# Three edits to a hybrid decoder block: attention emitted by pairs of query blocks, four weight sums moved to VectorE, a convolution split by token halves

## The chip, the cores and the metric

The kernel runs on one core of a Trainium2 chip. The metric is device microseconds of one execution; the runs before the change took 2504.47, 2507.64 and 2510.67 us, median 2507.64 us.

## The reference

One layer over 2048 tokens of width 1024, float32. What the change touches:

```python
hn = rmsnorm(x, g_mix);  proj = hn @ w_in            # LRU branch, gate branch, q, k, v
# causal depthwise convolution of width 4, then the recurrence with two block-diagonal gates
xc = sum(conv_w[k] * shift(x_lru, 3 - k) for k in range(4)) + conv_b
gate_r, gate_i = sigmoid(xc @ w_a + b_a), sigmoid(xc @ w_x + b_x)
h_t = a_t * h_{t-1} + sqrt(1 - a_t**2) * (gate_i * xc)_t;   y_lru = h * gelu(g_lru)
# attention: 16 heads of 64, blocks of 128 queries against the current and previous 128 keys, a sink per head
y_attn = softmax_with_sink(q @ k.T / 8, window=128) @ v
x = x + concat(rmsnorm(y_lru), rmsnorm(y_attn)) @ w_out
# squared-ReLU MLP
x = x + relu(rmsnorm(x) @ w_up)**2 @ w_down;   out = rmsnorm(x)
```

## The kernel before

The tokens are worked off in two chunks of 1024. A chunk goes through the input projection and attention, the recurrent group (LRU), the output projection, and the first half of the MLP; the second half of the MLP (w_down) follows for all tokens at the end. Matrix products take each float32 operand as a high part rounded by ScalarE (ACT) and a low part that VectorE (DVE) subtracts, so that a product is three TensorE (PE) matmuls: high-high, high-low, low-high. The MLP products use seven instead of eight block products, with sums of weight blocks and of activation blocks as operands.

The order of instructions on each engine is made at build time by a planner: it takes the instructions in the order in which the Python code emits them as their priority, simulates the engines with costs of its own, and gives each engine, when it is free, the ready instruction of highest priority. On the chip each engine then keeps that order and waits wherever its next instruction isn't ready. So the emission order sets priorities; it isn't the queue itself.

**Attention** (the loop over `s`, line 811 on). Step `s` makes the scores of head `s` and the probabilities and values of head `s-1`. A head has four pairs of query blocks. `scores(p)` does 4 matmuls into one of two PSUM buffers (`bank(0, ...)`, L629), DVE mixes the two key blocks (L637), takes the maximum (L639, L640), and ACT makes two exponentials (L643), which frees the buffer. `probs(p)` does 2 transposes (L662), ACT copies (L665), DVE subtracts (L666), GpSimd (POOL) masks twice (L669, L671). `values(p)` does 12 small matmuls (L686). `piece` is a quarter or an eighth of the projection of the next q, x or gate tile, the filler between them. Before the change the step runs in two halves: scores of two pairs, values of two pairs, probabilities of two pairs, two pieces.

**LRU.** For each of eight channel tiles `j`, `lru_a` convolves: ACT scales the two token halves of the projection (L740), DVE adds three shifted taps for each half (L747, L749), copies the last three columns aside (`halo`, L751), then ACT makes the high part `xhi` of all 1024 tokens (L754) and DVE the low part `xlo` (L755). `lru_b` multiplies both by the gate weights (L916 to L918), half by half.

**First half of the MLP.** `Up.run` starts pairs 0 and 1 of weight tiles together: two products each, then `sums()` (L364 to L368, with high parts by ACT L359 and low parts by DVE L360) makes the activation operands T4, T3, T1, then the rest of pair 0 and the rest of pair 1. `weight_sums` makes four half-width sums of the weights on POOL (L395 to L398), then splits them (L400 to L407). For pair 1 it is emitted behind the second of pair 0's remaining products.

Of the kernel before, what the change touches and what calls it, by code (L numbers as in the profile page):

```python
# [9 lines left out]
F32R = mybir.dt.float32r  # L10
# [3 lines left out]
AF = mybir.ActivationFunctionType  # L14
ALU = mybir.AluOpType
# [22 lines left out]
def hybrid_block_kernel(  # L38
# [16 lines left out]
    act = nc.scalar  # L55
    dve = nc.vector
# [18 lines left out]
    def f32(ap):  # L75
        return ap.bitcast(F32)
# [10 lines left out]
    def S(tag, name, dt=F32, shape=(P, D)):  # L87
        return slots.tile(list(shape), dt, name=name, tag=tag)

    def U(i, name, dt=F32, shape=(P, D)):  # L90
        return S(f"u{i}", name, dt, shape)
# [13 lines left out]
    def W(name, dt=F32R, shape=(P, D)):  # L105
        turn["w"] = (turn["w"] + 1) % 5
        return S(f"w{turn['w']}", name, dt, shape)
# [20 lines left out]
    HS = (slice(0, HALF), slice(HALF, D))  # L128
# [37 lines left out]
    def split_weight(src, at=None, eng=None, raw=None):  # L166

        if raw is None:
            raw = R("wraw")
            nc.sync.dma_start(raw, src)  # L170
        if at is None:
            hi, lo = W("whi"), W("wlo")
        else:
            hi, lo = U(at[0], "whi", F32R), U(at[1], "wlo", F32R)
        act.activation(hi, raw, AF.Copy)  # L175
        (eng or dve).tensor_tensor(lo, raw, f32(hi), op=ALU.subtract)  # L176
        return hi, lo
# [116 lines left out]
    pool = nc.gpsimd  # L294
    C_TAGS = ("u0", "u1", "u12")

    class Up:
# [91 lines left out]
            else:  # L389
                self.raws = r1, r2  # L390

        def weight_sums(self, fp, r1, r2):
            lo, hi = slice(0, HALF), slice(HALF, D)
            s12 = U(10, "s12", F32, (P, 2, HALF))
            pool.tensor_tensor(s12[:, 0], r2[:, lo], r2[:, hi], op=ALU.add)  # L395
            pool.tensor_tensor(s12[:, 1], s12[:, 0], r1[:, lo], op=ALU.subtract)
            pool.tensor_tensor(r2[:, lo], r1[:, lo], r2[:, lo], op=ALU.subtract)
            pool.tensor_tensor(r1[:, hi], r1[:, hi], s12[:, 1], op=ALU.subtract)  # L398
            s12h, s12l = W("s12h", F32R, (P, 2, HALF)), W("s12l", F32R, (P, 2, HALF))
            act.activation(s12h, s12, AF.Copy)  # L400
            dve.tensor_tensor(s12l, s12, f32(s12h), op=ALU.subtract)
            f2h, f2l = W("f2h"), U(20, "f2l", F32R)
            act.activation(f2h, r2, AF.Copy)  # L403
            dve.tensor_tensor(f2l, r2, f32(f2h), op=ALU.subtract)  # L404
            s4 = U(21, "s4", F32R, (P, 2, HALF))
            act.activation(s4[:, 0], r1[:, hi], AF.Copy)
            dve.tensor_tensor(s4[:, 1], r1[:, hi], f32(s4[:, 0]), op=ALU.subtract)  # L407
            self.ws[fp] |= {"S2": (s12h[:, 1], s12l[:, 1]), "S1": (s12h[:, 0], s12l[:, 0]),
                            "S3": (f2h[:, lo], f2l[:, lo]), "A22": (f2h[:, hi], f2l[:, hi]),
                            "S4": (s4[:, 0], s4[:, 1])}  # L410
# [66 lines left out]
        def run(self, ahead=None):  # L477
            c = self.c
            first = [self.pair(0), self.pair(1)]
            for i in range(2):  # L480
                if i == 1:
                    self.weights(1)
                for _ in range(2):
                    next(first[i])
            self.sums()
            for i in range(2):
                for n, _ in enumerate(first[i]):
                    if i == 0 and n == 1:
                        self.weight_sums(1, *self.raws)
                    if i == 1 and n == 0:  # L490
                        self.weights(2)
            steps = None
            for fp in range(2, NF // 2):
                for n, _ in enumerate(self.pair(fp, fp + 1 == NF // 2 and c + 1 < NCH)):
                    if n == 1 and fp + 1 < NF // 2:
                        self.weights(fp + 1)
                    if fp + 1 == NF // 2 and c + 1 < NCH:
                        if n == 0:
                            hn, steps = stage1(c + 1)
                        if n in (0, 2, 3, 4, 6):  # L500
                            next(steps)
                        if n == 4:
                            self.wkv = [split_weight(w_in[KT * 3 + i], at=(16 + 2 * i, 17 + 2 * i))
                                        for i in range(2)]
                    if ahead:
                        ahead(fp, n)
            self.next = (hn, steps) if steps else (None, None)
# [15 lines left out]
    for c in range(NCH):  # L523
# [204 lines left out]
        def lru_a(j, xps):  # L728
            def vcol(i):
                return vec[:, i, j:j + 1]  # L730

            wgr = small.tile([P, 2, HD], F32, name="wgr", tag="wgr", bufs=2)
            nc.sync.dma_start(wgr, w_gate[j])
            for s in range(2):
                s_ = slice(s * HD, s * HD + HD)
                act.activation(gd[s_, 0, :, s_], wgr[s_], AF.Copy)
                dve.tensor_tensor(gd[s_, 1, :, s_], wgr[s_], f32(gd[s_, 0, :, s_]), op=ALU.subtract)
            xc = U((16, 20)[j % 2], "xc")
            for n in range(2):
                act.activation(xc[:, HS[n]], xps[n], AF.Identity, scale=vcol(V_CW + 3), bias=vcol(V_CB))  # L740
            for n in range(2):
                before = xps[0][:, HALF - 3:] if n else halo[:, j, :]
                h0 = n * HALF
                for d in (1, 2, 3):
                    w = vcol(V_CW + 3 - d)
                    a_, b_ = slice(h0 + d, h0 + HALF), slice(h0, h0 + d)
                    dve.scalar_tensor_tensor(out=xc[:, a_], in0=xps[n][:, :HALF - d], scalar=w, in1=xc[:, a_],  # L747
                                             op0=ALU.mult, op1=ALU.add)
                    dve.scalar_tensor_tensor(out=xc[:, b_], in0=before[:, 3 - d:], scalar=w, in1=xc[:, b_],  # L749
                                             op0=ALU.mult, op1=ALU.add)  # L750
            dve.tensor_copy(halo[:, j, :], xps[1][:, HALF - 3:])  # L751
            xhi = U((17, 21)[j % 2], "xhi", F32R)
            xlo = U(18, "xlo", F32R)
            act.activation(xhi, xc, AF.Copy)  # L754
            dve.tensor_tensor(xlo, xc, f32(xhi), op=ALU.subtract)  # L755
            return [xc, xhi, xlo]

        def new_x(j):
# [39 lines left out]
        qs, yqs, heads, muls = {}, {}, {}, []  # L798
        pf_next = [0]
        late = []  # L800
        piece, done = new_q(0)
# [4 lines left out]
        piece, done = new_q(1)  # L806
# [4 lines left out]
        for s in range(NH + 1):  # L811
            j = s // 2

            free = mm("tp", (s + 1) // 2 % 2) if 0 < s < NH - 1 else None
            if s < NH:
                if s % 2 == 0:
                    yqs[j] = U(3 + j % 2, "yq", F32, (P, NT, P))
                heads[s] = Head(s, qs[j][s % 2], yqs[j])
            if s % 2 == 1:
                if j + 2 < KT:  # L820
                    piece, done = new_q(j + 2)
                else:
                    piece, done = (new_x if j + 2 == KT else new_gate)(0)

            for p0 in (0, 2):
                if s < NH:
                    for p in (p0, p0 + 1):
                        heads[s].scores(p)
                    if p0:
                        heads[s].sums()  # L830
                if len(late) == 4:
                    for _ in range(2):
                        heads[late[0][0]].values(late.pop(0)[1])
                if s > 0:
                    for p in (p0, p0 + 1):
                        heads[s - 1].probs(p, free)
                        late.append((s - 1, p))
                    if p0 and s % 2 == 1 and s > 1:
                        flip(j - 1, yqs[j - 1])
                for p in (p0, p0 + 1):  # L840
                    piece(p if s % 2 else 4 + p)
            if s % 2 == 1 and j + 2 < KT:
                done(0)
            if s % 2 == 0:
                if j + 1 < KT:
                    qs[j + 1] = done(1)
                elif j + 1 == KT:
                    lru_in = done()
                else:
                    lru_in.append(done())  # L850
# [121 lines left out]
        for grp in range(2):  # L972
# [5 lines left out]
            for k0, kn in (((0, 3), (3, 3), (6, 2)), ((0, 4), (4, 4)))[grp]:  # L978
# [6 lines left out]
                for t in range(NT):  # L985
                    n, tt = divmod(t, NT // 2)
# [336 lines left out]
```

## Time and profile before

| what | us |
|---|---|
| median of the three runs | 2507.64 |
| the profiled execution | 2507.72 |
| its span, first to last instruction | 2506.0 |
| PE busy | 2421.7 |
| DVE busy | 1762.8 |
| ACT busy | 1263.7 |
| POOL busy | 443.1 |

The span is what the profiler saw; the execution's time is 1.7 us longer. An engine's busy time excludes waits. PE is busy nearly all the time, so a change shows in the time only through PE's waits, through its granted clock, or through work that it does more or less of.

### The profile page before, as it was taken

What the parts mean: (1) busy time and instruction counts of PE and PEld (TensorE: products, weight loads), DVE (VectorE), ACT (ScalarE), POOL (GpSimd) and SP (SyncE); (2) the same over time, 40 slices, a digit from 0 to 9 for tenths busy, and PEclk for the clock granted to TensorE, in tenths of its full rate; (3) what the DMA queues carried; (4) which work ended last, traced back from release to release, by engine and by line L of the source; (5) the groups of instructions that cost most, each with busy time, mean ns of one, the idle gap of its engine ahead of it and who ended that gap; (6) DMA issues with size and microseconds to landing.
All of it is one profiled execution on the core that took longest, in us unless ns stands there. A gap on an engine that the chain in (4) does not pass through costs nothing. (4 is left out here: it accounts for less than half of the span.)

```text
span 2506.0 us, 32828 instructions
## 1 busy us (share of the span) xinstructions
PE 2421.7 (97%) x12338; PEld 1974.9 (79%) x12338; DVE 1762.8 (70%) x2534; ACT 1263.7 (50%) x2149; POOL 443.1 (18%) x455
## 2 busy tenths in 40 slices
PE   7999999999999999999999999999999999999997
PEld 6877777788788888877777788788878877888886
DVE  6788667856754556777676847655564898887888
ACT  6666777513455456665778315455454233322334
POOL 0344000001223210544000001423210110111100
PEclk9999999999999999999999999999999999999999
DMA  4111112412344444011113312444463454443424
GB/s 156 42 44 52 45 46 78 152 51 82 129 148 152 163 154 140 35 51 52 46 37 115 112 43 110 147 142 152 162 204 122 155 162 156 135 132 121 135 90 162
DMA packets 132815, 276.39 MB, mean 110 GB/s; under 512 B 11184, under 2 KB 70576, under 8 KB 132656
## 3 DMA queue, kind: packets, MB, share of 16 engines
q1 hardware_dynamic: 124880, 246.50, 29.3%
q0 software_dynamic: 5184, 18.88, 2.1%
q10 hardware_dynamic: 2592, 8.91, 0.9%
q8 instruction: 97, 1.59, 0.3%
q14 instruction: 62, 0.51, 0.1%
HBM read 190.37 MB, written 83.89 MB: 109 GB/s over the span
## 5 line engine op out<-in xcount | busy, mean ns | idle before, releaser
L1240 DVE TENSOR_TENSOR acc<-dd,acc 128x1024 f32<-128x1024 f32 x212 | 256.4, 1218 | 84.0 <-PE dd L1231 83.3
L997 PE MATMUL ops<-whi,ht 128*128 128x512 f32 x1024 | 280.0, 391 | 2.5 <-DVE halo L751 1.3
L1029 ACT ACTIVATE ah<-araw 128x1024 fp32r<-128x1024 f32 x96 | 102.0, 1063 | 299.3 <-PE dd L1231 286.7
L997 PEld LDWEIGHTS ops<-whi,ht 128*128 128x128 f32 x1024 | 191.3, 188 | 45.9 <-DVE x L1002 2.7
L997 PE MATMUL ops<-wlo,ht 128*128 128x512 f32 x512 | 159.2, 391 | 0.0
L669 POOL TENSOR_SCALAR_AFFINE_SELECT pf<-pf 128x512 f16<-128x512 f16 x128 | 89.0, 695 | 348.3 <-DVE pf L666 340.0
L175 ACT ACTIVATE whi<-wraw 128x1024 fp32r<-128x1024 f32 x84 | 88.5, 1055 | 120.6 <-PE ops L997 85.2
L404 DVE TENSOR_TENSOR f2l<-wraw,f2h 128x1024 fp32r<-128x1024 f32 x32 | 39.1, 1223 | 143.7 <-ACT f2h L403 143.7
L1030 DVE TENSOR_TENSOR al<-araw,ah 128x1024 fp32r<-128x1024 f32 x96 | 124.3, 1296 | 10.7 <-ACT ah L1029 10.7
L176 DVE TENSOR_TENSOR wlo<-wraw,whi 128x1024 fp32r<-128x1024 f32 x84 | 103.4, 1235 | 40.4 <-PE xps L234 14.5
L395 POOL TENSOR_TENSOR s<-wraw 128x512 f32<-128x512 f32 x32 | 41.5, 1296 | 500.9 <-DMA wraw<-in_w_up_dram 264.6
L643 ACT ACTIVATE st<-sc,mx 128x128 f32<-128x128 f32 x256 | 91.0, 366 | 62.8 <-DVE mx L640 62.1
L997 PEld LDWEIGHTS ops<-wlo,ht 128*128 128x128 f32 x512 | 95.6, 188 | 20.5 <-DVE wlo L176 1.2
L233 PE MATMUL qps<-ht,whi 128*128 128x512 f32 x256 | 105.4, 412 | 0.0
L403 ACT ACTIVATE f2h<-wraw 128x1024 fp32r<-128x1024 f32 x32 | 33.9, 1060 | 137.1 <-PE pa L417 132.9
L233 PE MATMUL xps<-ht,whi 128*128 128x512 f32 x256 | 101.5, 397 | 0.0
L234 PE MATMUL qps<-ht,whi 128*128 128x512 f32 x256 | 101.5, 396 | 0.0
L417 PE MATMUL qr<-hm,s 128*128 128x512 f32 x384 | 97.1, 401 | 4.3 <-DVE hid L456 4.3
L236 PE MATMUL qps<-ht,wlo 128*128 128x512 f32 x256 | 100.9, 394 | 0.0
L234 PE MATMUL xps<-ht,whi 128*128 128x512 f32 x256 | 100.9, 394 | 0.0
L233 PE MATMUL gpps<-ht,whi 128*128 128x512 f32 x256 | 100.5, 393 | 0.0
L234 PE MATMUL gpps<-ht,whi 128*128 128x512 f32 x256 | 100.0, 391 | 0.0
(334 smaller groups left out, 6843.1 us busy)
## 6 DMA issues: line engine op xcount, KB each, us to landing
araw<-act SPq DMA_DIRECT2D x96, 512.0 KB, 3.5
wraw<-in_w_up_dram SPq DMA_DIRECT2D x64, 512.0 KB, 3.2
act<-hid SPq DMA_DIRECT2D x128, 256.0 KB, 2.6
wraw<-in_w_in_dram SPq DMA_DIRECT2D x52, 512.0 KB, 3.2
act<-a SPq DMA_DIRECT2D x96, 256.0 KB, 2.7
wraw<-in_w_out_dram SPq DMA_DIRECT2D x32, 512.0 KB, 3.2
braw<-in_w_down_dram SPq DMA_DIRECT2D x28, 512.0 KB, 4.4
xt<-in_x_dram SPq DMA_DIRECT2D x16, 512.0 KB, 4.4
```

What stands on the lines that cost most here:

```text
L175: act.activation(hi, raw, AF.Copy)
L176: (eng or dve).tensor_tensor(lo, raw, f32(hi), op=ALU.subtract)
L233: pe.matmul(ps[m], w[0][:, k * P:(k + 1) * P], hk(ht[m][0], k), start=(k == 0), stop=False)
L234: pe.matmul(ps[m], w[0][:, k * P:(k + 1) * P], hk(ht[m][1], k), start=False, stop=False)
L236: pe.matmul(ps[m], w[1][:, k * P:(k + 1) * P], hk(ht[m][0], k), start=False, stop=(k == KT - 1))
L417: pe.matmul(ps, w[a_][:, ks], hk(h[b_], k), start=first and k == 0 and i == 0, stop=k == KT // 2 - 1 and i == 2, skip_group_check=True)
L643: ins = act.activation(self.st[:, b, :], cur[:, i, :], AF.Exp, bias=self.mx[:, b:b + 1], accum_out=self.ls[:, b:b + 1])
L669: nc.gpsimd.affine_select(out=pf[:, 1], in_=pf[:, 0], compare_op=ALU.is_gt, fill=0.0, base=0, pattern=[[0, 4], [-1, P]], channel_multiplier=1)
L997: pe.matmul(ps[m], a_, wk[k][b_][:, hs], start=(k == 0 and a_ is yh and b_ == 0), stop=(k == kn - 1 and a_ is ylo))
L1029: act.activation(hi, raw, AF.Copy)
L1030: dve.tensor_tensor(lo, raw, f32(hi), op=ALU.subtract)
L1240: dve.tensor_tensor(accs[blk][d_], o, accs[blk][d_], op=ALU.add)
```

## The change

Attention: the loop over halves becomes a loop over the four pairs, each with its scores, its probabilities and one piece; the values still come two pairs at a time, when four are waiting. MLP: `weight_sums` of pair 1, in each chunk, issues its four sums on DVE. Convolution: the high and low part of a token half are made right behind that half's taps; the copy of the last three columns is emitted behind both.

```diff
-        def weight_sums(self, fp, r1, r2):
+        def weight_sums(self, fp, r1, r2, eng=pool):
             lo, hi = slice(0, HALF), slice(HALF, D)
             s12 = U(10, "s12", F32, (P, 2, HALF))
-            pool.tensor_tensor(s12[:, 0], r2[:, lo], r2[:, hi], op=ALU.add)
-            pool.tensor_tensor(s12[:, 1], s12[:, 0], r1[:, lo], op=ALU.subtract)
-            pool.tensor_tensor(r2[:, lo], r1[:, lo], r2[:, lo], op=ALU.subtract)
-            pool.tensor_tensor(r1[:, hi], r1[:, hi], s12[:, 1], op=ALU.subtract)
+            eng.tensor_tensor(s12[:, 0], r2[:, lo], r2[:, hi], op=ALU.add)
+            eng.tensor_tensor(s12[:, 1], s12[:, 0], r1[:, lo], op=ALU.subtract)
+            eng.tensor_tensor(r2[:, lo], r1[:, lo], r2[:, lo], op=ALU.subtract)
+            eng.tensor_tensor(r1[:, hi], r1[:, hi], s12[:, 1], op=ALU.subtract)
...
                     if i == 0 and n == 1:
-                        self.weight_sums(1, *self.raws)
+                        self.weight_sums(1, *self.raws, eng=dve)
...
             xc = U((16, 20)[j % 2], "xc")
+            xhi = U((17, 21)[j % 2], "xhi", F32R)
+            xlo = U(18, "xlo", F32R)
...
                     dve.scalar_tensor_tensor(out=xc[:, b_], in0=before[:, 3 - d:], scalar=w, in1=xc[:, b_],
                                              op0=ALU.mult, op1=ALU.add)
+                act.activation(xhi[:, HS[n]], xc[:, HS[n]], AF.Copy)
+                dve.tensor_tensor(xlo[:, HS[n]], xc[:, HS[n]], f32(xhi[:, HS[n]]), op=ALU.subtract)
             dve.tensor_copy(halo[:, j, :], xps[1][:, HALF - 3:])
-            xhi = U((17, 21)[j % 2], "xhi", F32R)
-            xlo = U(18, "xlo", F32R)
-            act.activation(xhi, xc, AF.Copy)
-            dve.tensor_tensor(xlo, xc, f32(xhi), op=ALU.subtract)
...
-
-            for p0 in (0, 2):
+            for p in range(4):
                 if s < NH:
-                    for p in (p0, p0 + 1):
-                        heads[s].scores(p)
-                    if p0:
+                    heads[s].scores(p)
+                    if p == 3:
                         heads[s].sums()
                 if len(late) == 4:
                     for _ in range(2):
                         heads[late[0][0]].values(late.pop(0)[1])
                 if s > 0:
-                    for p in (p0, p0 + 1):
-                        heads[s - 1].probs(p, free)
-                        late.append((s - 1, p))
-                    if p0 and s % 2 == 1 and s > 1:
+                    heads[s - 1].probs(p, free)
+                    late.append((s - 1, p))
+                    if p == 3 and s % 2 == 1 and s > 1:
                         flip(j - 1, yqs[j - 1])
-                for p in (p0, p0 + 1):
-                    piece(p if s % 2 else 4 + p)
+                piece(p if s % 2 else 4 + p)
```

## Rows read from the trace of the kernel before

**Rows 1.** The page, busy time of an engine, share of the span, instructions.

```profile
PE 2421.7 (97%) x12338; PEld 1974.9 (79%) x12338; DVE 1762.8 (70%) x2534; ACT 1263.7 (50%) x2149; POOL 443.1 (18%) x455
```

**Rows 2.** PE's waits over the run: who waited for whom: us, times, longest.

```profile
PE sc L629 <- ACT st L643: 15.4, 26, 1.2
PE gps L916 <- ACT xhi L754: 7.9, 10, 0.9
```

**Rows 3.** Stretches: length, busy PE, PEld, DVE, ACT, POOL, granted clock, DMA, GB/s.

```profile
60.00:270.00 210.00, 198.45 (x1711) 165.34 (x1711) 163.61 (x433) 128.47 (x417) 87.30 (x136) 0.99 0.13 46
270.00:420.00 150.00, 145.76 (x631) 117.30 (x630) 101.72 (x149) 113.45 (x132) 0.00 (x0) 1.00 0.13 45
640.00:660.00 20.00, 16.29 (x55) 11.63 (x55) 17.65 (x15) 6.14 (x7) 5.97 (x4) 0.83 0.04 16
```

**Rows 4.** The same view, one period of two heads in the second chunk.

```profile
1082.00:1105.50 23.50, 21.85 (x207) 18.07 (x204) 18.91 (x48) 14.60 (x51) 10.16 (x17) 1.00 0.12 45
```

**Rows 5.** Timeline of that period: start, length, instruction [idle before <- releaser].

```profile
1088.47 1.48 DVE L176 TENSOR_TENSOR wlo<-wraw,whi 128x1024 fp32r<-128x1024 f32 x1
...
1090.33 1.39 DVE L608 SCALAR_TENSOR_TENSOR qs<-qps,qs 64x512 fp32r<-64x512 f32 x2
...
1092.20 0.43 DVE L637 COPY_PREDICATED sc<-prevm,sc 128x256 f32<-128x256 uint32 x1
...
1093.15 0.36 ACT L643 ACTIVATE st<-sc,mx 128x128 f32<-128x128 f32 x1
...
1093.66 1.53 PE L629 MATMUL sc<-kd,qs 128*128 128x256 f32 x8 [1.05 <-ACT st L643]
```

**Rows 6.** Timeline of the second chunk's LRU stage: one channel tile, then its end.

```profile
1275.67 1.43 ACT L740 ACTIVATE xc<-xps,vec 128x512 f32<-128x512 f32 x2
...
1276.94 0.74 DVE L747 SCALAR_TENSOR_TENSOR xc<-xps,vec,xc 128x511 f32<-128x511 f32 x1
...
1279.17 0.21 DVE L749 SCALAR_TENSOR_TENSOR xc<-halo,vec,xc 128x3 f32<-128x3 f32 x1
...
1285.44 1.06 ACT L937 ACTIVATE r<-yl 128x1024 f32<-128x1024 f32 x1 [5.01 <-DVE yl L933]
...
1288.31 1.05 ACT L754 ACTIVATE xhi<-xc 128x1024 fp32r<-128x1024 f32 x1
...
1289.41 0.74 PE L916 MATMUL gps<-xhi,gd 128*128 128x512 f32 x2 [0.83 <-ACT xhi L754]
...
1363.37 0.70 PE L997 MATMUL ops<-whi,ht 128*128 128x512 f32 x2 [0.65 <-DVE halo L751]
```

**Rows 7.** Timeline, splits of 512 columns.

```profile
1548.60 0.62 ACT L406 ACTIVATE s<-wraw 128x512 fp32r<-128x512 f32 x1
...
1549.26 0.69 DVE L407 TENSOR_TENSOR s<-wraw,s 128x512 fp32r<-128x512 f32 x1 [0.45 <-ACT s L406]
```

**Rows 8.** Timeline of the first chunk's MLP, pair 0 to pair 1.

```profile
638.22 0.62 PE L417 MATMUL pa<-hm,s12h 128*128 128x512 f32 x2
...
639.76 2.32 DVE L360 TENSOR_TENSOR hm<-braw,hm 128x1024 fp32r<-128x1024 f32 x1
...
658.20 0.66 PE L417 MATMUL pa<-hm,s12h 128*128 128x512 f32 x2
```

**Rows 9.** The same place in the second chunk.

```profile
1563.94 0.62 PE L417 MATMUL pa<-hm,s12h 128*128 128x512 f32 x2
...
1564.48 9.06 POOL L396 TENSOR_TENSOR s<-s,wraw 128x512 f32<-128x512 f32 x1
...
1565.50 1.22 DVE L360 TENSOR_TENSOR hm<-braw,hm 128x1024 fp32r<-128x1024 f32 x1
...
1574.55 2.30 DVE L360 TENSOR_TENSOR hm<-t,hm 128x1024 fp32r<-128x1024 f32 x1
...
1576.91 0.49 PE L417 MATMUL qr<-hm,s12h 128*128 128x512 f32 x1 [0.78 <-DVE hm L360]
...
1579.71 0.63 PE L417 MATMUL pa<-hm,s12h 128*128 128x512 f32 x2
```

## The prediction

> **What bounds the kernel now.** I read the busy times first: PE is busy for 2421.7 of 2506.0 us, 97%, DVE for 70% [rows 1]. So no more than 84.3 us of waits can come back, and no other engine is near its limit over the whole run. Next, PE's waits by releaser: the two largest inside the edited code are the score matmuls waiting for ACT's exponentials to free a score buffer, 15.4 us in 26 waits, and the gate matmuls waiting for ACT's `xhi`, 7.9 us in 10 waits [rows 2]. Third, the stretches. Attention of the first chunk has 210.00 - 198.45 = 11.6 us without PE, the LRU stretch 4.2 us, and the 20 us around the weight sums 3.7 us at a granted clock of 0.83 of full, so part of them at the lower of the two levels (1.2 instead of 2.4 GHz) [rows 3]. A clock that falls costs beyond idle time, because the matmuls themselves become longer; no busy share shows that.
>
> **Attention by pairs.** No instruction is added or removed; the order changes. The timeline of one regular period of 23.5 us (two heads; PE 21.85, DVE 18.91, ACT 14.60 busy [rows 4]) shows the mechanism. The eight score matmuls of two pairs fill both buffers together; the next eight can start only when the first pair's second exponential ends, at 1093.15 + 0.36 = 1093.51. In front of that exponential on DVE's queue stood a weight's low part (1.48), two query splits (1.39) and the key mix of the *second* pair (0.43). PE came 1.05 us too early [rows 5]. By pairs, the second pair's scores are issued behind a transpose pair and six projection matmuls, so its key mix cannot stand in front of the first pair's maximum, and the second pair's buffer is wanted a quarter step later. The first buffer comes free 0.4 earlier, so this wait falls from 1.05 to about 0.6; if the planner also moves the query splits behind the first pair's chain (1.39 us more), it is gone. The waits below 1 us should go, as the lead gained on the second buffer exceeds them. I take two thirds of 15.4: 10.3 us back. The ends: all 15.4; or nothing, and each of 64 added changes from transposes to projections (two more in each of 16 steps of two chunks) costs 0.1 us, as a first matmul behind a break lasts 0.49 [rows 9] where one in a stream lasts 0.62 - 0.23 = 0.39 (145.76 us for 631 is 0.23 a step [rows 3, 9]): 6 us lost. No wait precedes these changes, which is what lengthened that matmul, so I take 1 us. Attention: -9.
>
> What is late next there is DVE itself: 18.91 us of work in a period that shrinks towards 22.2, 85%. Its instructions are short, but two long ones in a row (1.48 + 1.39) are still longer than a quarter step.
>
> **Weight sums on DVE.** The four POOL sums of pair 1 run beside the splits of `sums()`, and the two engines hold each other up. In the first chunk DVE's low part of T4 took 2.32 us where 1.22 is the time of the same line alone; in the second, one POOL sum was held for 9.06 us while DVE ran at 1.22, and the next two then made DVE's T1 part take 2.30 [rows 8, 9]. The price is seen between the same two products, pair 0's S2 and pair 1's S2: 658.20 - 638.22 = 20.0 us in the first chunk, 1579.71 - 1563.94 = 15.8 in the second [rows 8, 9]. Same matmuls, so the first chunk loses 4.2 us more, part in waits, part at the lower clock (0.83 over the 20 us [rows 3]). In the second chunk at least the 0.78 us wait for the stretched T1 part goes too [rows 9]. Without POOL beside it I expect 15.0 in both: 5.0 + 0.8 = 5.8 us back.
>
> What it adds: four DVE instructions of 512 columns from SBUF, at 0.69 each from the split of that shape [rows 7], 2.8 us per chunk. They are emitted behind all of `sums()`, so by priority they queue behind the T3 and T1 parts; behind them wait the low part of the next pair's A11, pair 0's first activation sum and pair 1's own weight splits. In the second chunk DVE would reach them near 1575.2 and leave them near 1578, about when ACT needs them, so this hides, barely. If the planner puts them in front of T3's or T1's low parts, PE waits 2.8 us a chunk, 5.6 in all, and nothing is won. Bounds -8 (the waits left in the second chunk go as well) to 0; I take -6.
>
> **Convolution by halves.** In the tile shown, the taps of the first half ended at 1279.38, yet `xhi` started at 1288.31, because it is one instruction over both halves; PE waited 0.83 us for it [rows 6]. ACT stood idle for 5.01 us before 1285.44 [rows 6], so the first half's `xhi` fits there. The dependence is kept by region and not by tile: the first tap on half 0 began at 1276.94, while ACT still wrote half 1 until 1277.10 [rows 6]. The second half's `xhi` takes 0.62 instead of 1.05 [rows 6, 7] and ends near 1288.9; `xlo` follows in 0.69, until about 1289.6 [rows 7]. PE is there at 1288.58, has the first half's three matmuls to do (0.23 each, 0.7 us), and then meets a second half that is nearly ready: 0.1 us is left of 0.83. Ten such waits: 7 us back; I take -6, as the planner may place the gate matmuls earlier on the strength of the earlier operands.
>
> It adds 16 instructions to each of two engines: 2 x 0.62 - 1.05 = 0.19 us on ACT, 2 x 0.69 - 1.22 = 0.16 on DVE [rows 6, 7, 9]. They hide, as ACT is busy for 113.45 of 150.00 us there, 76%, DVE for 68% [rows 3]; without that cover they cost 16 x 0.35 = 5.6 us. The `halo` copy is now emitted behind the second `xlo`. The output projection waited 0.65 us for it [rows 6]; if DVE really does it last, that wait grows by ACT's 0.62 and DVE's 0.69 and whatever ACT has in front, up to some 3 us per chunk. I cost it at nothing: the copy is ready before `xlo` and the planner gives a free engine what is ready. Bounds for the whole part: -8 to +12 (5.6 + 6).
>
> Here the row and a rule of the Trainium skill can part. The row says that ACT and DVE have a quarter to a third of the LRU stretch free [rows 3], so two short instructions are as good as one long. The page Perfetto Trace Analysis, section Optimizing Scalar/DVE Operations, states a fixed cost per instruction for either engine and advises larger operations where the engine is saturated; it also advises breaking up where an engine only causes bubbles elsewhere. By the first half of that rule this edit would be a loss of the added time, by the second a gain.
>
> **Sum.** Against the profiled execution's own 2507.72 us (span 2506.0 and 1.7 around it, 0.1 from the median 2507.64): -9 - 6 - 6 = -21, so 2487 us.
>
> **Rivals.**
> *DVE binds attention.* The score waits turn into waits for DVE, which has 18.91 us of work in 23.5 [rows 4]. For it: the two long DVE instructions remain in every period. Against: it leaves 4.6 us free, and the waits are due to order. Attention gains nothing: -12, 2496 us.
> *Slower: the chain of a single pair.* With pairs the PE queue has its two score points a quarter step apart, and at each the exponential of two pairs ago must have ended. Where DVE's 1.48 and 1.39 fall between the two, the second point waits as well as the first, with nothing but six matmuls (1.4 us) to cover 2.9 us. If that happened once in each of the 64 old half steps at 0.35 us, attention would lose 22 us instead of gaining 9, against 12 from the other two edits: +10, 2518 us. It decides from 12 / 64 = 0.19 us per half step. Against it: each buffer's own turnaround is as long as before.
> *The halves run into ACT.* ACT's queue holds table loads, and a half `xhi` queued in front of them makes everything behind it wait for the taps. Then the split costs its 5.6 us instead of giving 6: 2498 us. The rule on saturated engines would have it so.
> *All goes.* The score waits vanish whole, the clock holds, the gate waits vanish: -15 - 8 - 8 = -31, and a few waits of other kinds in attention with them: 2474 us.
>
> **Chances.** The forecast 0.50, DVE binds 0.18, halves 0.10, all goes 0.10, slower 0.12. A difference within 0.3%, 7.5 us, can't be told from no change. Around the forecast the parts' bounds give 2478 to 2496. The two middle rivals fall mostly on the faster side of 2500; about a third of them, and a little of the forecast, falls within 7.5 us of before. So faster 0.77, same 0.12, slower 0.11. For 8 in 10 I take 2473 to 2504, which leaves out the slower case and half of no change.
>
> **What would show it.** PE's waits for the score buffers fall from 15.4 to some 5 us, and PE's idle time in a period of attention from 1.65 to about 1.1 or less. The span from pair 0's S2 to pair 1's S2 is near 15 us in both chunks, with no DVE split above 1.3 us and a granted clock of 1.00 there. The gate matmuls' waits for `xhi` sum to 1 or 2 us, and the output projection waits for `halo` no longer than 0.7. The prediction is wrong if waits of like size reappear under DVE's mask subtraction (L666) or key mix (L637), if the weight sums stand ahead of T1's low parts on DVE, or if ACT shows idle time in front of the first half's `xhi`.

## The result and the profile after

The changed kernel runs in 2477.07 us, median of four runs (2475.98 to 2479.82), beside 2507.56 for the kernel before in the same comparison: ratio 0.988, 95% interval [0.9863, 0.9897]. It is 30.5 us faster, where 21 were forecast, and inside the range. The profiled execution took 2475.98 us with a span of 2474.3, so 31.7 us went out of the span.

The page after, busy time of the engines, against [rows 1]:

```profile
PE 2407.7 (97%) x12338; PEld 1973.1 (80%) x12338; DVE 1762.4 (71%) x2558; ACT 1272.8 (51%) x2165; POOL 432.5 (17%) x447
```

PE's busy time fell by 14.0 us for the same 12338 matmuls. The other 17.7 us are idle time (84.3 before, 66.6 after). PE's waits after, against [rows 2] (engine, tile and line, releaser: us, times, longest; the shorter attention loop moves the lines of `lru_b` up by four):

```profile
PE sc L629 <- ACT st L643: 11.2, 24, 1.6
...
PE sqt L724 <- POOL accq L934: 4.1, 2, 2.0
PE gps L912 <- ACT xhi L753: 2.3, 2, 1.2
...
PE gps L912 <- ACT r L915: 1.7, 2, 0.8
PE gps L913 <- DVE xlo L754: 1.4, 2, 0.7
```

Three more of the list before:

```profile
PE tp L662 <- DVE pf L666: 2.6, 5, 1.5
...
PE sqt L724 <- POOL accq L938: 1.6, 2, 1.0
PE ops L997 <- DVE halo L751: 1.3, 2, 0.7
```

The score waits fell by 4.2 only, those for `xhi` by 5.6, and the transposes of the LRU's sum of squares (`sqt`) now wait 4.1 for POOL, before 1.6. The waits of attention's transposes (`tp`) and those for `halo` are gone from the list after.

Attention of either chunk, from its first score matmul to its last value matmul, as a stretch of the trace before and of the trace after (columns as in [rows 3]):

```profile
65.72:259.00 193.28, 181.87 (x1632) 152.00 (x1631) 157.46 (x424) 119.76 (x406) 86.76 (x135) 0.99 0.12 45
991.30:1184.66 193.36, 183.11 (x1631) 150.53 (x1630) 149.66 (x382) 118.85 (x401) 85.49 (x135) 1.00 0.12 45
```

```profile
65.61:252.02 186.41, 177.24 (x1626) 148.98 (x1625) 157.66 (x425) 122.09 (x407) 90.83 (x135) 1.00 0.13 46
978.21:1159.12 180.91, 176.01 (x1625) 148.79 (x1624) 151.09 (x383) 121.19 (x402) 90.32 (x135) 1.00 0.13 48
```

Both became shorter, by 6.9 and 12.4 us. Six projection matmuls, 1.36 us a chunk, lie behind the last value matmul after the change (x1626 against x1632); less these, attention gained 5.5 and 11.1, in all 16.6 us. In the second chunk at a granted clock of 1.00 in both traces, idle time fell from 10.25 to 4.90 us and PE's busy time by 7.10, of which 1.36 are the six matmuls: 5.7 us of the gain lay in time that counted as busy. Over both chunks idle time fell by 7.6 us, and the other 9.0 of the 16.6 lay in busy time (in the first chunk the clock went from 0.99 to 1.00 as well).

Three more stretches after: the 20 us from pair 0's S2 on, one period of two heads, and the LRU stretch of [rows 3]:

```profile
631.35:651.35 20.00, 18.38 (x78) 13.87 (x77) 19.01 (x21) 10.04 (x12) 4.24 (x2) 1.00 0.08 26
1053.16:1074.90 21.74, 21.06 (x200) 18.02 (x200) 18.85 (x48) 14.79 (x51) 11.22 (x18) 1.00 0.14 50
270.00:420.00 150.00, 147.29 (x642) 119.53 (x641) 104.03 (x159) 117.55 (x142) 0.00 (x0) 1.00 0.15 50
```

Around the weight sums the clock is 1.00 where it was 0.83. The period went from 23.50 to 21.74 us and its idle time from 1.65 [rows 4] to 0.68. From score matmul to score matmul the period before holds 200 matmuls too; the window of [rows 4] is cut elsewhere and counts 207.

Weight sums: the S2 products (those with the weight sum `s12h`) of pairs 0 and 1, first and second chunk, in the timeline of PE after, and DVE's queue between the first two:

```profile
631.35 0.62 PE L417 MATMUL pa<-hm,s12h 128*128 128x512 f32 x2
...
645.69 0.73 PE L417 MATMUL pa<-hm,s12h 128*128 128x512 f32 x2 [0.60 <-ACT s12h L400]
...
1536.75 0.61 PE L417 MATMUL pa<-hm,s12h 128*128 128x512 f32 x2
...
1551.06 0.73 PE L417 MATMUL pa<-hm,s12h 128*128 128x512 f32 x2 [0.58 <-ACT s12h L400]
```

```profile
641.46 1.22 DVE L360 TENSOR_TENSOR hm<-t,hm 128x1024 fp32r<-128x1024 f32 x1
642.60 0.69 DVE L395 TENSOR_TENSOR s<-wraw 128x512 f32<-128x512 f32 x1
643.20 0.69 DVE L435 TENSOR_TENSOR hid<-pb,sc 128x512 f32<-128x512 f32 x1
...
645.00 0.69 DVE L398 TENSOR_TENSOR wraw<-wraw,s 128x512 f32<-128x512 f32 x1
```

From S2 to S2 it is 14.34 and 14.31 us, before 19.98 and 15.77 [rows 8, 9]: 7.1 less. Every quarter split takes 1.22. The sums stand behind T1's low part, and PE now waits 0.6 for the split of their result.

LRU after: a channel tile of the first chunk, then the end of the stage, where the last tile's sum of squares is added on POOL:

```profile
297.60 0.61 ACT L753 ACTIVATE xhi<-xc 128x512 fp32r<-128x512 f32 x1
303.69 1.06 ACT L933 ACTIVATE r<-yl 128x1024 f32<-128x1024 f32 x1 [5.47 <-DVE yl L929]
304.77 1.28 ACT L786 ACT_TABLE_LOAD   x1
306.06 0.60 ACT L786 ACTIVATE ge<-gpps 128x512 f32<-128x512 f32 x1
306.56 0.62 ACT L753 ACTIVATE xhi<-xc 128x512 fp32r<-128x512 f32 x1
...
307.23 0.50 PE L912 MATMUL gps<-xhi,gd 128*128 128x512 f32 x1 [1.16 <-ACT xhi L753]
...
455.54 2.35 POOL L934 TENSOR_TENSOR accq<-accq,r 128x1024 f32<-128x1024 f32 x1 [1.65 <-ACT r L933]
457.94 1.19 PE L724 MATMUL sqt<-ident,accq 128*128 128x128 f32 x8 [2.02 <-POOL accq L934]
```

The first half's `xhi` goes early, into ACT's idle time. The second half's stands behind a table load and a gelu, as the whole `xhi` of [rows 6] did before. From attention's last value matmul to the MLP's first product the chunks gained 1.2 and 3.0 us, the six moved matmuls taken into account.

So the 31.7 us of the span are: attention 16.6, S2 to S2 7.1, from there to pair 2's S2 2.3 (0.8 and 1.5), LRU to MLP 4.2, all else 1.5.

### The profile page after: what moved, and what is told of

The parts are those of the page before. It is cut to its first block, busy times and chain, and to the rows that moved or that the text cites. A ratio compares the mean times of both kernels' runs of the same rounds, so it can differ in the third digit from the quotient of the medians.

```text
span 2474.3 us, 32801 instructions
## 1 busy us (share of the span) xinstructions
PE 2407.7 (97%) x12338; PEld 1973.1 (80%) x12338; DVE 1762.4 (71%) x2558; ACT 1272.8 (51%) x2165; POOL 432.5 (17%) x447
## 4 chain that ended last, share of the span: by engine, by line
PE 66%; DVE 16%; issue 8%; ACT 7%; DMA 1%; POOL 1%; POOLq 0%; SPq 0%; DVEq 0%; ACTq 0%
PE dd L1227 15%; PE ops L993 12%; PE qr L417 10%; PE pa L417 9%; PE pb L417 3%; PE xps L234 2%; PE xps L233 2%; PE sc L629 2%; PE xps L236 2%; DVE acc L1236 2%; DVE qs L608 1%; DVE wlo L176 1%; PE gpps L233 1%; PE gpps L234 1%; PE gpps L236 1%
## 5 line engine op out<-in xcount | busy, mean ns | idle before, releaser
L176 DVE TENSOR_TENSOR wlo<-wraw,whi 128x1024 fp32r<-128x1024 f32 x84 | 106.1, 1268 | 23.8 <-ACT whi L175 10.3
```

## Experiments

All times are medians beside runs of the kernel before on the same chip.

**Attention alone.** The kernel before with the loop over four pairs.

```diff
-            for p0 in (0, 2):
+            for p in range(4):
```

> The kernel before with the attention loop by pairs alone. Theory (the stretches from landmark to landmark say that attention gives 16 to 17 us, of which 4 are fewer waits for the score buffers and the rest is time that the trace counts as busy matmuls): -15 to -18 us, about 2491. Rival (part of what stands in the attention stretch comes from the convolution's earlier parts, which attention's last steps also emit): -8 to -11 us, about 2498, near what the list of waits allowed.

Measured: 2487.63 against 2507.48, ratio 0.9923 [0.9909, 0.9936], 19.9 us less, more than either theory said. Attention became shorter by 5.96 and 10.77 us, 16.7 together, as in the whole change and as the first theory has it, with score waits at 11.1. The rest is the first chunk's S2 to S2, 15.75 instead of 19.98, though the weight sums are untouched and both queues keep their order there: POOL's second sum is now held for 9.06 us, as in the second chunk before [rows 9], while DVE runs at 1.22. What differs is when they began.

**Weight sums alone.**

```diff
-                        self.weight_sums(1, *self.raws)
+                        self.weight_sums(1, *self.raws, eng=dve)
```

> The kernel before with pair 1's four weight sums on VectorE alone. Theory (the two engines hold each other up, and that is all that is undone): -8 to -10 us, about 2498, with no VectorE split of sums() over 1.3 us. Rival (the stretch from S2 to S2 became shorter because attention and convolution left other engines further ahead): -4 to -6 us, about 2502.

Measured: 2500.47 against 2507.48, 0.9975 [0.9965, 0.9985], 7.0 us less, between the two theories. S2 to S2 is 14.33 and 14.31, 7.1 less, as in the whole change: the other two edits add nothing to this stretch.

**Convolution alone.**

```diff
+                act.activation(xhi[:, HS[n]], xc[:, HS[n]], AF.Copy)
+                dve.tensor_tensor(xlo[:, HS[n]], xc[:, HS[n]], f32(xhi[:, HS[n]]), op=ALU.subtract)
```

> The kernel before with the convolution and its split by halves alone. Theory (waits for xhi go, but three waits of about 1 us per chunk and a longer wait for the sum of squares before the output projection come in their place): -3 to -5 us, about 2504. Rival (the prediction's 6 us, or more, as the planner gets ready operands earlier): -6 to -8 us, about 2500.

Measured: 2498.32 against 2507.48, 0.9963 [0.995, 0.9975], 9.2 us less, more than either theory said. The stretches share it otherwise than the number suggests: LRU to MLP gained 2.65 and 4.1, S2 to S2 went to 15.75 (4.2 less) and 17.65 (1.9 more), without an edit there. Waits for `xhi` fell to 2.3, those for the sum of squares rose to 4.1. In the second chunk, POOL's and then DVE's queue of this kernel:

```profile
1554.07 2.16 POOL L396 TENSOR_TENSOR s<-s,wraw 128x512 f32<-128x512 f32 x1
...
1558.42 2.25 POOL L398 TENSOR_TENSOR wraw<-wraw,s 128x512 f32<-128x512 f32 x1
```

```profile
1555.00 2.32 DVE L360 TENSOR_TENSOR hm<-braw,hm 128x1024 fp32r<-128x1024 f32 x1
...
1559.47 2.29 DVE L360 TENSOR_TENSOR hm<-braw,hm 128x1024 fp32r<-128x1024 f32 x1
```

Here the engines take turns and DVE's three instructions lose 1.1 us each; in the kernel before at the same place POOL was held for 9.06 us and DVE ran on [rows 9]. The granted clock of this S2 to S2 is 0.90, in the kernel before 1.00.

**Attention and weight sums.** Both edits, the convolution as before.

```diff
+            for p in range(4):
...
+                        self.weight_sums(1, *self.raws, eng=dve)
```

> The changed kernel with the convolution as before. If the three edits add up: 2477 plus the convolution's share, 2480 to 2482. If the convolution is worth nothing or harms beside the other two: 2477 or less. If it is worth the prediction's 6 us: 2483.

Measured: 2481.10, 0.9895 [0.9881, 0.9908], 26.4 us less. So the convolution brings the last 4.0; the intervals of the two kernels overlap, but from attention's first score to the MLP the traces have 0.9 and 3.4 us of it. The three parts alone sum to 36.1, 5.6 more than the whole: the first chunk's S2 to S2 became 4 to 6 us shorter in each of them, and can do so once.

**Scores by pair, the rest by twos.** The changed kernel; probabilities and values go back to twos.

```diff
-            for p in range(4):
+            for p0 in (0, 2):
                 if s < NH:
-                    heads[s].scores(p)
...
+                    heads[s].scores(p0)
...
+                    for p in (p0, p0 + 1):
+                        heads[s - 1].probs(p, free)
+                        late.append((s - 1, p))
...
+                piece(p0 if s % 2 else 4 + p0)
+                if s < NH:
+                    heads[s].scores(p0 + 1)
...
+                piece(p0 + 1 if s % 2 else 5 + p0)
```

> The changed kernel, but in attention only the scores are spread: each half step has one pair's scores, the values, the probabilities of two pairs, one piece, the other pair's scores, one piece. Theory (the gain comes from the score buffers: the second pair's key mix no longer stands in front of the first pair's maximum, and its scores no longer wait for the second buffer): within 3 us of the changed kernel, 2477 to 2480. Rival (the gain comes from spreading transposes, copies and masks over the step): 2488 or more.

Measured: 2473.17 against 2506.59, 0.9868 [0.9852, 0.9885]. PE's wait list of it:

```profile
PE sc L629 <- ACT st L643: 7.1, 13, 1.6
```

Attention takes 187.52 and 180.00 us, 5.8 and 13.4 below the kernel before: the scores' spacing alone gives all that the changed kernel gains there, and in the second chunk 2.3 more. The whole is below what the theory said; its interval overlaps that of the changed kernel, so that it is the faster of the two rests on the stretches.

**Probabilities by pair, scores by twos.**

```diff
-            for p in range(4):
+            for p0 in (0, 2):
                 if s < NH:
-                    heads[s].scores(p)
+                    for p in (p0, p0 + 1):
+                        heads[s].scores(p)
...
+                for p in (p0, p0 + 1):
+                    if s > 0:
+                        heads[s - 1].probs(p, free)
...
+                    piece(p if s % 2 else 4 + p)
```

> The changed kernel, but in attention the scores come two pairs at a time as before and only probabilities and pieces are spread. Theory of the score buffers: nearly all of attention's 16.7 us is lost, 2490 to 2494. Rival (spreading of the probabilities): within 3 us of the changed kernel, 2477 to 2480.

Measured: 2488.87, 0.9927 [0.9912, 0.9942], near the theory of the score buffers (2490 to 2494) and far from its rival; attention 192.19 and 190.98 us, 1.1 and 2.4 below the kernel before. Its wait list:

```profile
PE sc L629 <- ACT st L643: 15.4, 23, 1.4
```

So the score waits go with two pairs of scores in a row, not with where the transposes stand.

**Weight sums ahead of `sums()`.** On DVE as in the change, but issued before T4, T3 and T1.

```diff
+            self.s12_early = self.four_sums(*self.raws, dve)
             self.sums()
```

> The changed kernel, but the four weight sums of pair 1 are emitted in front of sums() instead of behind, so that by priority they come ahead of the splits of T4, T3 and T1 on VectorE, once their weights have landed. The prediction's bound: PE then waits up to 2.8 us a chunk more, 2480 to 2483, and the stretch from S2 to S2 grows from 14.3 towards 17. Rival (VectorE has slack in front of the T parts, or the weights land so late that the order hardly moves): 2477, the stretch stays at 14.3.

Measured: 2478.80, 0.9889 [0.9874, 0.9904], below the 2480 to 2483 of the bound and not told apart from the changed kernel by the intervals; S2 to S2 16.28 in both chunks, against 14.3. DVE has the four sums, of which these are the first and the last, in front of T4's first low part:

```profile
630.13 0.67 DVE L395 TENSOR_TENSOR s<-wraw 128x512 f32<-128x512 f32 x1
...
633.07 0.68 DVE L398 TENSOR_TENSOR wraw<-wraw,s 128x512 f32<-128x512 f32 x1
```

Without its cover the work on DVE costs 2.0 of its 2.8 us per chunk.

**Idle work on GpSimd.** The changed kernel with four additions on POOL that nobody needs, free to start when y2 is whole.

```diff
+            s3 = small.tile([P, HALF], F32, name="s3", tag="s3", bufs=1)
+            for q in range(4):
+                pool.tensor_tensor(s3, self.y2[0][:, 0], self.y2[1][:, q % 2], op=ALU.add)
             self.sums()
```

> The changed kernel with four more additions on GpSimd that nobody needs (128x512, of the sum y2 into a scratch tile), free to start when y2 is whole, that is beside VectorE's quarter splits between the second first-pair products S2. Theory, that VectorE's two-input operations and GpSimd's slow each other whatever they compute: several quarter splits (lines 360, 368) at 2.2 to 2.4 us against 1.22, or a GpSimd addition held 5 to 9 us; the stretch from the first pair's S2 to the second pair's 16 to 19 us against 14.3, the whole 2 to 8 us slower than the changed kernel, 2479 to 2485. Rival, that in the kernel before only the chain behind GpSimd's late sums cost time: splits at 1.2 and the stretch at 14.3, the whole within 1 us of 2477.

Measured: 2483.68 against 2506.51, 0.9907 [0.9893, 0.9922]; S2 to S2 17.59 and 17.58, all as the theory has it. POOL's queue of this kernel, then DVE's:

```profile
627.11 7.92 POOL L487 TENSOR_TENSOR s<-y,y 128x512 f32<-128x512 f32 x4 [44.61 <-DVE y L344]
```

```profile
628.09 3.48 DVE L348 TENSOR_TENSOR hm<-y,hm 128x512 fp32r<-128x512 f32 x2
...
633.83 2.29 DVE L360 TENSOR_TENSOR hm<-braw,hm 128x1024 fp32r<-128x1024 f32 x1
636.04 1.21 DVE L368 TENSOR_TENSOR braw<-y,braw 128x1024 f32<-128x1024 f32 x1
```

While POOL runs, the quarter split of 1.21 takes 2.29, and the two instructions of L348 take 3.48, where they took 1.28 in the kernel with the sums first; L364 between them, at 632.69, keeps its 1.21, and behind POOL all is 1.21 again. Nothing waits for these additions, so DVE's price comes from POOL's working beside it, not from a late result.

**The last sum of squares on DVE.**

```diff
-                (dve if j + 1 < KT else nc.gpsimd).tensor_tensor(accq, accq, r_, op=ALU.add)
+                dve.tensor_tensor(accq, accq, r_, op=ALU.add)
```

> The changed kernel, but the last channel tile's sum of squares is added by VectorE like the other seven instead of by GpSimd. PE waits 2.0 us in each chunk for that add. Theory (GpSimd's add of 2.35 us is the end of that chain): half to all of the 4.1 us comes back, 2473 to 2475. Rival (the chain in front of it, scan, product and square, is late already, or VectorE's add is queued behind the splits): 2476 to 2478.

Measured: 2472.72 against 2506.59, 0.9864 [0.9849, 0.9878]. The wait of its transposes fell from 4.1 to 1.5 and LRU to MLP by 2.4 and 0.6. The median is 4.4 us below the changed kernel's, with intervals that overlap; the two stretches give 3.0 of it. The later tail was part of what the convolution by halves lost.

**Scores by pair and that sum together.** Both edits on the changed kernel, as shown above.

```diff
+                    heads[s].scores(p0)
...
+                dve.tensor_tensor(accq, accq, r_, op=ALU.add)
```

> The changed kernel with the scores alone going pair by pair (probabilities and projection by twos, as before), and the last sum of squares of the recurrence on VectorE instead of GpSimd. Theory, that the two gains lie in different stretches and are off each other's path: the changed kernel's 2477.1 less 3 to 4 from the scores and less 3 to 4 from the sum of squares, so 2469 to 2472, ratio to the kernel before 0.985 to 0.986, TensorE waits for the scores' exponentials about 7 us and the wait of the squares' transposes for the sum 1.5 us. Rival, that either run's surplus was the same 2.7 us per chunk (which of two engines comes first at the weight sums): 2472.5 to 2474, no better than either alone.

Measured: 2470.17 against 2506.51, 0.9852 [0.9837, 0.9867], as the first theory has it and the fastest median of all; from either edit alone it can't be told apart by the intervals. Attention takes 187.49 and 179.98 us. The stretch of the second chunk:

```profile
973.75:1153.73 179.98, 178.43 (x1632) 149.35 (x1631) 146.98 (x383) 120.58 (x402) 81.68 (x135) 1.00 0.14 48
```

Only 1.55 us without PE are left there. In the first chunk score waits of 6.7 stay; which instructions hold them wasn't tried.

**The same with the whole convolution.**

```diff
-                act.activation(xhi[:, HS[n]], xc[:, HS[n]], AF.Copy)
-                dve.tensor_tensor(xlo[:, HS[n]], xc[:, HS[n]], f32(xhi[:, HS[n]]), op=ALU.subtract)
...
+            act.activation(xhi, xc, AF.Copy)
+            dve.tensor_tensor(xlo, xc, f32(xhi), op=ALU.subtract)
```

> The same as the run beside it (scores by pair, weight sums and the last sum of squares on VectorE), with the convolution and its split undone: both halves convolved, then one whole xhi and one whole xlo. It gives the convolution's own worth when the end of the recurrence no longer hangs on GpSimd. Theory, that the convolution by halves was worth the 6 us forecast and lost 2.5 of it at the recurrence's end: slower than the run beside it by 5 to 7 us, TensorE waits of the gates for xhi 7 to 8 us against 2.3. Rival, that its gain is taken by the activation-table load and the gelu in front of the second half in any case: slower by 3 to 4 us, with the waits for xhi as many but other waits after them shorter.

Measured: 2478.23, 0.9887 [0.9872, 0.9901], so 8.1 us slower than the run beside it, more than either theory said. Its wait list:

```profile
PE gps L916 <- ACT xhi L754: 9.0, 12, 1.1
```

From attention's first score to the MLP, undoing the halves costs 4.8 and 4.4 us. Both theories took too little: beside scores by pair and that sum on DVE, the halves are worth twice the 4.0 that they bring in the changed kernel.

## Why the prediction was right or wrong

The direction and the three mechanisms held. Two terms were near and one was far too small.

**Attention, forecast -9, measured -16.6.** The step that failed is "I take two thirds of 15.4: 10.3 us back." It failed twice. The listed score waits gave back 4.2, not 10.3; and a wait list was taken as the whole loss, so that the gain went beyond the part's own end of 15.4. From start to start it looks different. In a stream a 512-column matmul begins 0.23 us after the one ahead but its row lasts 0.39, as here in the timeline after:

```profile
1071.00 0.39 PE L234 MATMUL qps<-ht,whi 128*128 128x512 f32 x1
1071.23 0.39 PE L236 MATMUL qps<-ht,wlo 128*128 128x512 f32 x1
```

The next one may therefore be 0.16 late before any idle time shows, and each listed wait is short by as much. Counted over the second chunk's attention, in excess of each kind's spacing in a stream (the shortest tenth of its gaps), late starts by more than 0.08 us under such cover fell from 261 to 208 and all such cover from 30.12 to 24.05 us. These 6.1 us and the 5.35 of idle time make up the 11.1 measured, to 0.4. Not all of this cover is waiting: 19.0 us before and 17.5 after lie at matmuls that wait for no semaphore, mostly transposes one behind another. At matmuls that wait for one it fell from 11.1 to 6.6, so some 4.5 of the 6.1 us are waits that the list doesn't show. A score matmul's row "x8 1.53" [rows 5] held such time as well.

Of the details, the key mix of the second pair did leave its place in front of the first pair's maximum, and the query splits stayed there. Timeline after:

```profile
1072.36 1.39 DVE L608 SCALAR_TENSOR_TENSOR qs<-qps,qs 64x512 fp32r<-64x512 f32 x2
...
1073.78 0.23 DVE L640 TENSOR_SCALAR mx<-mx,snk 128x2 f32<-128x2 f32 x1
...
1074.04 0.37 ACT L643 ACTIVATE st<-sc,mx 128x128 f32<-128x128 f32 x1 [1.29 <-DVE mx L640]
...
1074.38 0.42 DVE L637 COPY_PREDICATED sc<-prevm,sc 128x256 f32<-128x256 uint32 x1
...
1074.90 0.74 PE L629 MATMUL sc<-kd,qs 128*128 128x256 f32 x4 [0.50 <-ACT st L643]
```

The wait of 1.05 became 0.50; 0.6 had been worked out. Of the period's eight places where scores are asked for, two still wait, 0.7 us together. The microsecond for changes of matmul kind wasn't isolated; but with the whole convolution, scores and probabilities by pair take 182.56 us in the second chunk and scores alone 178.50 with six matmuls (1.36 us) fewer, so the finer interleaving of the rest costs 2.7 us there, and 2.3 with the convolution by halves. The first chunk gained 5.6 us less than the second. Part of it is that it had less to lose: three regular periods took 22.62 to 22.99 us there before and 23.50 in the second chunk, after the change 21.87 and 21.75. The rest is open.

**Weight sums, forecast -6, measured -7.1 from S2 to S2.** The stretch was put at 15.0 and came to 14.3 in each chunk. The order on DVE was as said: behind T1's low parts, no split above 1.3, clock 1.00. That the work hides only barely shows in PE's wait of 0.6 for the split of its result; ahead of `sums()` it costs 2.0 us a chunk. What the step missed is that "the first chunk loses 4.2 us more" was no property of the first chunk: either other edit alone turned it over (15.75 us), so that 4.2 of the 7.1 came with each of them as well. That the term came near is in part luck.

**Convolution, forecast -6, measured -4.2 in its stretch.** Waits for `xhi` fell by 5.6, near the 6 forecast. The halo, cost at nothing, cost nothing: its wait is gone from the list. The added 16 instructions hid, with ACT busy for 117.55 of 150 us. What was left out is what comes late next: `sqt` waits 2.5 longer, as the last tile's sum is on POOL, and the waits for `xlo` and `r` are 2.7 longer. With the convolution by halves these two are on the list only where scores and probabilities both go by pair, and not in the runs with the convolution alone, the scores alone or the probabilities alone by pair. Why, wasn't pursued. Of the rule of the Trainium skill in Perfetto Trace Analysis, Optimizing Scalar/DVE Operations, the second half holds here: smaller pieces helped, and neither engine was saturated (ACT busy for 78% of the stretch after, DVE for 69%).

**Rivals.** DVE didn't bind attention: 18.85 us in a period of 21.74, and 1.55 us of PE idle time left in the best version's second chunk. The chain of a single pair cost nothing on the whole: attention became shorter in both chunks. The halves did run into ACT, though not at 5.6 us: in one tile of each chunk the second half came 1.16 us late behind a table load and a gelu, and ACT's idle time in front of `xhi`, 10.7 us over the run, lies nearly all (9.8) in front of second halves, until the taps and the `halo` copy behind them were done; in front of first halves, where the prediction had a sign against itself, it is under 1 us:

```profile
L753 ACT ACTIVATE xhi<-xc 128x512 fp32r<-128x512 f32 x32 | 20.1, 628 | 10.7 <-DVE halo L755 9.8 <-DVE xc L751 0.8
```

"All goes" (2474) was nearest in size, though not by its reason: the score waits stayed at 11.2, and more than half of attention's gain lay where no wait is listed. The prediction's narrow band, 2478 to 2496, isn't what its parts' bounds add up to: -31.4 to +18 us, 2476 to 2526.

## What to carry to other kernels

In attention here the list of waits was a lower bound of what an order costs: take the time from start to start over one period and compare it with the same instructions in a stream, since up to 0.16 us of every late start counted as busy time; and set apart the gaps at instructions that wait for nothing. With two score buffers, spacing their users evenly was the whole of attention's gain, and interleaving the other work more finely took some of it back. When an edit removes a late wait, price the next instruction in line too, and do not credit to an edit a race between two engines that another start time can decide otherwise.

## What was unexpected of the hardware

DVE and POOL, each on operands in SBUF, do not share evenly nor always to the same one's cost: in turns both take 2.2 to 2.3 us instead of 1.2 and 1.3, or POOL is held for 9.06 us while DVE runs at 1.22 [rows 9]. The same instructions in the same order gave 15.8 to 20.0 us from S2 to S2, with other start times. In the kernel before, POOL's second sum began 0.17 us behind DVE's L364 in the first chunk, and they took turns; in the second it began 0.11 behind [rows 9], and was held:

```profile
638.63 1.21 DVE L364 TENSOR_TENSOR braw<-braw,y 128x1024 f32<-128x1024 f32 x1
638.80 2.19 POOL L396 TENSOR_TENSOR s<-s,wraw 128x512 f32<-128x512 f32 x1
...
1564.37 1.21 DVE L364 TENSOR_TENSOR braw<-braw,y 128x1024 f32<-128x1024 f32 x1
```

The Trainium skill, SBUF — State Buffer, section Who interferes with whom, states that a DVE instruction with two inputs in SBUF contends with a POOL instruction that reads SBUF, that the shared ports are an exclusive lock, and that the order of issue decides who blocks. The traces agree with the turns of 2.2 to 2.3; a hold of 9.06 us over several DVE instructions is longer than one instruction's lock, and by the traces, in which spans on POOL are rough, DVE had begun first in both cases above. What decides between turns and hold stays open.
